# Attention weights turned by 32x32 blocks inside SBUF on SyncE's queue, and queries and keys turned before the values are projected

## The chip, the cores and the metric

One core of one Trainium2 chip runs the whole kernel: TensorE (PE in the profile), VectorE (DVE), ScalarE (ACT), GpSimd (POOL) and SyncE (SP), with 16 DMA engines. SyncE computes nothing here: it issues transfers, in the order in which they stand in its queue, and waits ahead of each for what that transfer needs. GpSimd issues the other transfers in the same manner. The metric is the time of one execution on the device, in microseconds.

## The reference, cut to what matters

One encoder block on 512 tokens (8 rows of 64) of width 1024, all in float32: a half-step SwiGLU feed-forward, a mixer, and a second half-step feed-forward. The mixer projects to seven parts and joins two branches, a gated recurrence and a neighbourhood attention with 16 heads of 64:

```python
xr, gr, q, k, v, ga, gb = jnp.split(h @ w_in[l], splits, axis=-1)
q = _rmsnorm(q.reshape(B_, S, N_HEADS, HEAD_DIM), q_norm[l]) * (HEAD_DIM ** -0.5)
k = _rmsnorm(k.reshape(B_, S, N_HEADS, HEAD_DIM), k_norm[l])
# per row of tokens: an 8 x 32 window of keys for each block of 16 columns, masked to 16
p = jax.nn.softmax(s + bias, axis=-1);  o = p @ v
y = jax.nn.sigmoid(ga) * y_lru + jax.nn.sigmoid(gb) * y_att
x = x + y @ w_out[l]
```

## The kernel before, in words

Every matrix product is made exact enough by splitting both operands into a high and a low part: a block of weights of 512 KB (a chunk) is loaded into `wraw` (three buffers), its high part `wh` is written by ACT or, for every other gate chunk, by DVE (lines 145 and 147), its low part `wl` by DVE (line 148); `wh` and `wl` have four buffers each. A chunk then feeds 24 matmuls of 128x512. So a load can be issued once the chunk three before it has been split, and a chunk can be split once TensorE is done with the chunk four before it. All chunk loads stand on SyncE's queue.

The middle of the kernel goes: projection of xr (8 chunks); then for each half of the heads (hf 0 and 1) a group of 4 chunks for q, 4 for k, 4 for v (24 `wqkv` chunks); then 24 `wg` chunks for the three gates; then 8 `wout` chunks. Each q, k or v group holds all four `acc` banks of PSUM until its results have been copied out: q and k by ACT (line 843), v by DVE (line 856). The next group's matmuls need these banks.

Beside this stream two lanes are woven in, coroutines that advance a few steps after each chunk: the recurrence ("lru") and the attention ("att", the function `heads`). For one half of the heads the attention does the following.

- Norm and turn: the factors `rq` from the sums of squares (lines 894 to 899), then for each of 8 blocks a multiply (904) and a 32x32 block transpose (906) on DVE, and 4 transfers from POOL's queue to DRAM (909): 32 of them in a half.
- `fetch`: reading q and k back in head-major order, as tile `xqk`, on SyncE's queue (917), two transfers for two heads pairs.
- `start(fi)`, for one pair of heads of four: high and low parts of q and k, the last of which is `kl` (939). The scores need it.
- `scores`: 12 matmuls for two of the four column blocks (a unit, n2 = 0 or 1), then on DVE bias and maximum (982), on ACT the exponential (989), on DVE the division (991, 994). In the first half a unit is one step, in the second half both units of a pair go together.
- `ship(fi, n2)`: the weights of a unit have to be transposed for the next matmul. DVE transposes 32x32 blocks into `pt` (1003, 1004; one buffer), one transfer writes `pt` to DRAM as `pd`, and four read it back with blocks exchanged, as `PT` (1006, 1010; three buffers). All five stand on POOL's queue, which waits for the write ahead of the reads.
- `apply(fi)`: 32 matmuls of `PT` with the values (1024), two units after the scores; its result goes to ACT (1034) and, in the gate stage, into y (1103).

The order on every engine is fixed ahead of the run by a list scheduler from the program's order, priorities, and when buffers come free in its own reckoning. On the chip each engine takes its instructions in that order and waits at the first one that is not ready.

Of the kernel before, what the change touches and what calls it, by code (L numbers as in the profile page):

```python
# [9 lines left out]
F32 = mybir.dt.float32  # L10
F32R = mybir.dt.float32r
AF = mybir.ActivationFunctionType
ALU = mybir.AluOpType
# [3 lines left out]
P = 128  # L17
T = 512
# [5 lines left out]
HD = 64  # L24
EPS = 1e-6
ROWS, GW = 8, 64
NCB, QC = 4, 16
# [64 lines left out]
def block_kernel(ctx: ExitStack, tc, a, out):  # L92
    nc = tc.nc
# [3 lines left out]
    big = ctx.enter_context(tc.tile_pool(name="big", bufs=1))  # L97
# [3 lines left out]
    dram = ctx.enter_context(tc.tile_pool(name="dram", bufs=1, space=bass.MemoryType.DRAM))  # L101
# [6 lines left out]
    def nm(s):  # L108
        uid[0] += 1
        return f"{s}_{uid[0]}"  # L110

    NBIG = 43

    def big_t(dt=F32, shape=(P, T), n="b"):
        return big.tile(list(shape), dt, tag="big", bufs=NBIG, name=nm(n))

    def pair_t():
        return big.tile([P, 2, T], F32, tag="pair", bufs=4, name=nm("pair"))
# [132 lines left out]
    def hold(i):  # L251

        after(i, mark["mm"])
        return i
# [12 lines left out]
    def make_forms(xg):  # L267


        half = T // 2  # L270
        F, S = {}, {n: [] for n in FORMS}

        def raw(n, k):
            if k % 2 == 0:
                F[n, k // 2] = big_t(n=n, shape=(P, 2, half))
            x1, x2 = xg[k], xg[k + 4]
            f = F[n, k // 2][:, k % 2]
            if n == "s1":
                sub(f, x2[:, half:], x1[:, half:])
            elif n == "s2":  # L280
                sub(f, F["s1", k // 2][:, k % 2], x1[:, :half], True)
            elif n == "s4":
                sub(f, F["s2", k // 2][:, k % 2], x2[:, :half], True)
            else:
                sub(f, x1[:, :half], x1[:, half:])

        def cut(n):
            H, L = (big_t(F32R, n=n, shape=(P, 2, half)) for _ in range(2))
            mark["cut", n] = split(F[n, len(S[n]) // 2], H, L)
            S[n] += [(H[:, i], L[:, i]) for i in range(2)]  # L290

        return S, raw, cut
# [529 lines left out]
    def tok_group(w, hf):  # L822
        pss = [acc_t() for _ in range(NCB)]
        for kp in range(4):
            H, L = load_w(a["wqkv"][w * 2 + hf, kp], 1024)
            for j in range(NCB):
                tj = slice(j * P, (j + 1) * P)
                for k in range(2):
                    kk = kp * 2 + k
                    s = slice(k * T, (k + 1) * T)  # L830
                    nc.tensor.matmul(pss[j], xh[kk][:, tj], H[:, s], start=kk == 0, stop=False)  # L831
                    nc.tensor.matmul(pss[j], xl[kk][:, tj], H[:, s], start=False, stop=False)  # L832
                    mark["mm"] = nc.tensor.matmul(pss[j], xh[kk][:, tj], L[:, s], start=False, stop=kk == KT - 1)  # L833
            if kp < 3:
                weave(RATE[phase[0]])
        return pss

    def qk_raw(w, hf, st):
        raws = []
        for ps in tok_group(w, hf):  # L840
            t = big_t(n="qk")
            with tc.high_priority():
                copy = nc.scalar.activation(t, ps, AF.Copy)  # L843
            raws.append(t)
        for j, t in enumerate(raws):
            sq = big_t(n="sq")
            after(nc.scalar.activation(sq, t, AF.Square), copy)
            nc.vector.reduce_sum(st[:, w, j, :], sq.rearrange("p (h d) -> p h d", d=HD), axis=AX.X)
        weave(RATE[phase[0]])
        return raws  # L850

    def v_get(hf):
        for j, ps in enumerate(tok_group(2, hf)):
            t = big_t(n="v")
            with tc.high_priority():
                nc.vector.tensor_scalar(t, ps, rcol[:, j : j + 1], None, ALU.mult)
            V[hf, 2 * j] = t

        for j in range(NCB):
            nc.gpsimd.dma_start(vd[hf][:, j * QC : (j + 1) * QC, :], V[hf, 2 * j])  # L860
        for j in range(3):
            t = big_t(n="vs")
            nc.gpsimd.dma_start(t, vd[hf][:, j * QC + 8 : j * QC + 24, :])
            V[hf, 2 * j + 1] = t


        for n, (own, single) in EDGE.items():
            ta, te = big_t(n="va"), big_t(n="ve")
            nc.gpsimd.memset(te, 0.0)
            for h in range(2):  # L870
                for t, half, g in ((ta, 0, own[h][0]), (ta, 1, own[h][1]), (te, h, single)):
                    c = KSTART[n] + g * 8
                    nc.gpsimd.dma_start(
                        t[half * HD : (half + 1) * HD].rearrange("p (f h d) -> p f h d", h=2, d=HD)[:, :, h],
                        vd[hf][:, c : c + 8, :].rearrange("r c (f h d) -> r c f h d", h=2, d=HD)[:, :, :, h])
            V[hf, "own", n], V[hf, "single", n] = ta, te
        weave(RATE[phase[0]])
# [8 lines left out]
            if g == 0:  # L886
                after(ld, mark["xr"])

    def heads(hf, raws, st):

        xs = {}
        qd = [dram.tile([P, NCB, NCB, P], F32, tag="qd", bufs=4, name=nm("qd")) for _ in range(2)]
        rq = tiny.tile([P, 2, NCB, 8], F32, tag="rq", name=nm("rq"))
        for w in range(2):
# [2 lines left out]
                                             ALU.mult, ALU.add))  # L897
        hold(nc.scalar.activation(rq, rq, AF.Sqrt))
        nc.vector.reciprocal(rq, rq)
        yield  # L900
        for w in range(2):
            for j in range(NCB):
                t = raws[w][j].rearrange("p (h d) -> p h d", d=HD)
                hold(nc.vector.tensor_tensor(t, t, rq[:, w, j, :].unsqueeze(2).to_broadcast([P, 8, HD]), ALU.mult))
                t2 = big_t(n="qkt")
                nc.vector.transpose(
                    t2.rearrange("p (c f i) -> p f c i", c=NCB, i=32), raws[w][j].rearrange("p (f c i) -> p f c i", c=NCB, i=32))
                for ab in range(NCB):
                    nc.gpsimd.dma_start(
                        qd[w].rearrange("(c i) j a x -> j a i c x", c=NCB)[j, ab],  # L910
                        t2[ab * 32 : (ab + 1) * 32].rearrange("p (c x) -> p c x", c=NCB))
            yield

        def fetch(g):
            for w in range(2):
                x = big.tile([P, 16, 2, 32], F32, tag="xqk", bufs=2, name=nm("xqk"))
                nc.sync.dma_start(
                    x.rearrange("p x f i -> p x (f i)"), qd[w].rearrange("p j a (g x) -> g p (j a) x", g=2)[g])
                for f in range(2):
                    xs[w, g * 2 + f] = x[:, :, f]  # L920

        yield
        fetch(0)
        yield
        qk, rss, soft, PTs = {}, {}, {}, {}
# [71 lines left out]
        def ship(fi, n2):  # L997

            outer, inner = soft.pop((fi, n2))
            t = big.tile([P, NCB, 7, 32], F32, tag="pt", bufs=1, name=nm("pt"))  # L1000
            sub = lambda b, n: b[:, : n * P].rearrange("p (q c i) -> p q c i", q=n, i=32)
            to = t.rearrange("p c q i -> p q c i")
            nc.vector.transpose(to[:, 4:], sub(outer, 3))
            nc.vector.transpose(to[:, :4], sub(inner, 4))
            d = dram.tile([P, NCB, 7 * 32], F32, tag="pd", bufs=4, name=nm("pd"))
            nc.gpsimd.dma_start(d, t.rearrange("p c q i -> p c (q i)"))
            PT = big.tile([P, NCB, 7, 32], F32, tag="PT", bufs=3, name=nm("PT"))
            for j in range(4):
                q = slice(j * 32, (j + 1) * 32)
                nc.gpsimd.dma_start(PT[:, j].rearrange("p q i -> p (q i)"), d[q].rearrange("i c x -> c i x"))  # L1010
            PTs[fi, n2] = PT.rearrange("p a q i -> p q a i")

        def apply(fi, behind=None):
# [30 lines left out]
        for i in range(len(units) + LC):  # L1044
            behind = None
            if i < len(units):
                fi, n2s = units[i]
                behind = scores(fi, n2s)
            if i >= LC and 1 in units[i - LC][1]:
                apply(units[i - LC][0], behind)  # L1050
            if i < len(units):
                for n2 in n2s:
                    ship(fi, n2)
                if 0 in n2s:
                    if fi < 3:
                        start(fi + 1)
                    if hf * 4 + fi + 1 < KT:
                        bias(hf * 4 + fi + 1)
            yield
            if phase[0] == "g":  # L1060
                yield
                yield
# [4 lines left out]
    for hf in range(2):  # L1067
        st = tiny.tile([P, 2, NCB, 8], F32, tag="st", name=nm("st"))
        raws = [qk_raw(0, hf, st), qk_raw(1, hf, st)]
        v_get(hf)  # L1070
        lanes["att"].append(heads(hf, raws, st))
        phase[0] = "t1" if hf == 0 else "g"


# [144 lines left out]
```

## Time and profile before

| | |
|---|---|
| Three runs | 1209.34, 1210.40, 1210.51 us; median 1210.4 us |
| Profiled execution | 1211.51 us, of which the span is 1209.7 us |
| Busy: PE, PE weight loads, DVE, ACT, POOL | 1112.6, 983.2, 823.9, 582.4, 197.6 us |
| Mean granted clock of TensorE | 0.953 of full |
| Queues | SP's 32.3% of the 16 engines' time, POOL's 23.0% |

Times in the trace are counted from the span's start. Both feed-forward blocks, 0 to about 350 us and from 864 us on, keep TensorE busy nearly without a gap. The mixer lies between them. A busy TensorE can run at half clock, which the column PEclk of the windows shows.

### The profile page before, as it was taken

The numbers are of one execution on the slowest core, as the hardware profiler recorded it, in microseconds if no ns is written. First come the engines' busy times: TensorE is split into PE (matmuls) and PEld (weight loads), VectorE is DVE, ScalarE is ACT, GpSimd is POOL, SyncE is SP. The second block draws the span as 40 slices with busy tenths as digits, with TensorE's granted clock in tenths as the row PEclk, the third lists the DMA queues.
The fourth block names the chain that finished last, engine by engine and source line by source line (L and its number), as shares of the span: only waits on it lengthen the run. The fifth ranks groups of instructions, "written<-read, shape, count | busy, mean of one in ns | idle before, by whom it ended". The sixth has DMA issues, their size and how long they took to land. (4 is left out here: it accounts for less than half of the span.)

```text
span 1209.7 us, 17700 instructions
## 1 busy us (share of the span) xinstructions
PE 1112.6 (92%) x6747; PEld 983.2 (81%) x6747; DVE 823.9 (68%) x1312; ACT 582.4 (48%) x874; POOL 197.6 (16%) x331
## 2 busy tenths in 40 slices
PE   9999999999999999897869962468999999999998
PEld 8899999988887788686658852356999999998887
DVE  7777878866558679966456586424987777775552
ACT  8545454644436697643333224214655454554340
POOL 0000000000003403713532052330100000000000
PEclk9999999999999999899879985588999999999999
DMA  8566666634236947658455365355766666663330
GB/s 269 151 157 158 157 158 157 162 100 132 81 112 161 259 117 228 165 165 233 134 150 167 106 188 136 92 167 147 181 189 161 152 163 153 162 172 108 100 110 35
DMA packets 82149, 184.33 MB, mean 152 GB/s; under 512 B 32656, under 2 KB 36496, under 8 KB 82064
## 3 DMA queue, kind: packets, MB, share of 16 engines
q1 hardware_dynamic: 56256, 122.50, 32.3%
q0 software_dynamic: 25232, 60.44, 23.0%
q8 instruction: 53, 0.87, 0.3%
q10 hardware_dynamic: 576, 0.26, 0.1%
q14 instruction: 32, 0.26, 0.1%
HBM read 154.72 MB, written 19.92 MB: 144 GB/s over the span
## 5 line engine op out<-in xcount | busy, mean ns | idle before, releaser
L145 ACT ACTIVATE wh<-wraw 128x1024 fp32r<-128x1024 f32 (+3 forms) x224 | 220.7, 988 | 344.0 <-issue 98.9
L148 DVE TENSOR_TENSOR wl<-wraw,wh 128x1024 fp32r<-128x1024 f32 (+3 forms) x236 | 267.3, 1137 | 109.5 <-ACT wh L145 108.4
L312 PE MATMUL acc<-s,wh 128*128 128x256 f32 x1280 | 232.2, 283 | 0.0
L312 PEld LDWEIGHTS acc<-s,wh 128*128 128x128 f32 x1280 | 199.7, 192 | 0.0
L312 PE MATMUL acc<-s,wl 128*128 128x256 f32 x640 | 181.1, 283 | 0.0
L312 PEld LDWEIGHTS acc<-s,wl 128*128 128x128 f32 x640 | 122.9, 192 | 0.0
L172 PE MATMUL acc<-xh,wh 128*128 128x512 f32 x272 | 109.6, 403 | 0.0
L174 PE MATMUL acc<-xh,wl 128*128 128x512 f32 x272 | 108.3, 398 | 0.0
L173 PE MATMUL acc<-xl,wh 128*128 128x512 f32 x272 | 108.1, 397 | 0.0
L312 PE MATMUL acc<-xh,wl 128*128 128x256 f32 x320 | 90.6, 283 | 0.0
L312 PE MATMUL acc<-xl,wh 128*128 128x256 f32 x320 | 90.6, 283 | 0.0
L312 PE MATMUL acc<-xh,wh 128*128 128x256 f32 x320 | 90.5, 283 | 0.0
L831 PE MATMUL acc<-wh,xh 128*128 128x512 f32 x192 | 76.5, 399 | 4.9 <-ACT qk L843 4.9
L832 PE MATMUL acc<-wh,xl 128*128 128x512 f32 x192 | 75.7, 394 | 0.0
L833 PE MATMUL acc<-wl,xh 128*128 128x512 f32 x192 | 75.6, 394 | 0.0
L148 DVE TENSOR_TENSOR hl<-h,hh 128x512 fp32r<-128x512 f32 x88 | 57.2, 687 | 21.8 <-PE aux L173 21.5
L172 PE MATMUL aux<-hh,wh 128*128 128x512 f32 (+1 forms) x181 | 69.9, 386 | 0.0
L173 PE MATMUL aux<-hl,wh 128*128 128x512 f32 (+1 forms) x181 | 69.9, 386 | 0.0
L174 PE MATMUL aux<-hh,wl 128*128 128x512 f32 (+1 forms) x181 | 69.9, 386 | 0.0
L173 PE MATMUL acc<-hl,wh 128*128 128x512 f32 (+1 forms) x176 | 67.9, 386 | 0.0
L174 PE MATMUL acc<-hh,wl 128*128 128x512 f32 (+1 forms) x176 | 67.9, 386 | 0.0
L172 PE MATMUL acc<-hh,wh 128*128 128x512 f32 (+1 forms) x176 | 67.9, 386 | 0.0
(222 smaller groups left out, 2374.1 us busy)
## 6 DMA issues: line engine op xcount, KB each, us to landing
wraw<-wqkv SPq DMA_DIRECT2D x24, 512.0 KB, 5.3
wraw<-wg SPq DMA_DIRECT2D x24, 512.0 KB, 3.9
wraw<-w1d SPq DMA_DIRECT2D x22, 512.0 KB, 3.7
wraw<-w2s SPq DMA_DIRECT2D x22, 512.0 KB, 4.2
pair<-w2s SPq DMA_DIRECT2D x22, 512.0 KB, 5.3
wraw<-w2d SPq DMA_DIRECT2D x22, 512.0 KB, 3.6
wraw<-w1s SPq DMA_DIRECT2D x18, 512.0 KB, 4.0
pair<-w1s SPq DMA_DIRECT2D x18, 512.0 KB, 5.5
```

The source lines that it names most:

```text
L145: nc.scalar.activation(H, raw, AF.Copy)
L148: return nc.vector.tensor_tensor(L, raw, H.bitcast(F32), ALU.subtract)
L172: nc.tensor.matmul(ps, wh, xh, start=first, stop=False, skip_group_check=skip)
L173: nc.tensor.matmul(ps, wh, xl, start=False, stop=False, skip_group_check=skip)
L174: mark["mm"] = nc.tensor.matmul(ps, wl, xh, start=False, stop=last, skip_group_check=skip)
L312: mm = nc.tensor.matmul(o, w_[:, c], x_, start=first and m + k == 0 and w_ is H and x_ is xh_, stop=m + k == 4 and w_ is L, skip_group_che ...
L831: nc.tensor.matmul(pss[j], xh[kk][:, tj], H[:, s], start=kk == 0, stop=False)
L832: nc.tensor.matmul(pss[j], xl[kk][:, tj], H[:, s], start=False, stop=False)
L833: mark["mm"] = nc.tensor.matmul(pss[j], xh[kk][:, tj], L[:, s], start=False, stop=kk == KT - 1)
```

## The change: what it does

- `ship` no longer goes through DRAM. The 4x4 grid of 32x32 blocks is exchanged by 16 transfers from SBUF to SBUF, each of 32 partitions by 224 values (28 KB), on SyncE's queue instead of POOL's five. There are 16 units in the kernel, so 256 such transfers take the place of 80. `ship` is given high priority.
- Norm, turn and store of q and k leave the coroutine and stand, as `turn_qk`, ahead of the projection of v; the multiplies lose the tie (`hold`) that kept them behind the newest matmul. `heads` begins with `fetch` and so needs three steps fewer before its first scores.
- New tiles: 43 shared tiles of 2 KB become 38; eight slots of 4 KB ("quad") hold, one after the other in the program, the split forms of the feed-forward, the first half's raw q and k, `xqk`, `pt` and `PT`, which had 2, 1 and 3 buffers of their own.

```diff
-    NBIG = 43
+    NBIG = 38
...
+    def quad_t(shape, dt=F32, n="quad"):
+        return big.tile(list(shape), dt, tag="quad", bufs=8, name=nm(n))
...
         def cut(n):
-            H, L = (big_t(F32R, n=n, shape=(P, 2, half)) for _ in range(2))
+            t = quad_t((P, 2, 2, half), F32R, n)
+            H, L = t[:, 0], t[:, 1]
...
     def qk_raw(w, hf, st):
         raws = []
-        for ps in tok_group(w, hf):
-            t = big_t(n="qk")
+        for j, ps in enumerate(tok_group(w, hf)):
+            if hf == 1:
+                t = big_t(n="qk")
+            else:
+                if j % 2 == 0:
+                    both = quad_t((P, 2, T), n="qk")
+                t = both[:, j % 2]
...
-    def heads(hf, raws, st):
-
-        xs = {}
+    def turn_qk(raws, st):
+
         qd = [dram.tile([P, NCB, NCB, P], F32, tag="qd", bufs=4, name=nm("qd")) for _ in range(2)]
...
         nc.vector.reciprocal(rq, rq)
-        yield
         for w in range(2):
             for j in range(NCB):
                 t = raws[w][j].rearrange("p (h d) -> p h d", d=HD)
-                hold(nc.vector.tensor_tensor(t, t, rq[:, w, j, :].unsqueeze(2).to_broadcast([P, 8, HD]), ALU.mult))
+                nc.vector.tensor_tensor(t, t, rq[:, w, j, :].unsqueeze(2).to_broadcast([P, 8, HD]), ALU.mult)
...
-            yield
+        return qd
+
+    def heads(hf, qd):
+
+        xs = {}
...
-                x = big.tile([P, 16, 2, 32], F32, tag="xqk", bufs=2, name=nm("xqk"))
+                x = quad_t((P, 16, 2, 32), n="xqk")
...
-        yield
         fetch(0)
...
         def ship(fi, n2):
...
-            t = big.tile([P, NCB, 7, 32], F32, tag="pt", bufs=1, name=nm("pt"))
+            t = quad_t((P, NCB, 7, 32), n="pt")
...
-            d = dram.tile([P, NCB, 7 * 32], F32, tag="pd", bufs=4, name=nm("pd"))
-            nc.gpsimd.dma_start(d, t.rearrange("p c q i -> p c (q i)"))
-            PT = big.tile([P, NCB, 7, 32], F32, tag="PT", bufs=3, name=nm("PT"))
-            for j in range(4):
-                q = slice(j * 32, (j + 1) * 32)
-                nc.gpsimd.dma_start(PT[:, j].rearrange("p q i -> p (q i)"), d[q].rearrange("i c x -> c i x"))
+            PT = quad_t((P, NCB, 7, 32), n="PT")
+            for i in range(4):
+                for j in range(4):
+                    nc.sync.dma_start(PT[i * 32 : (i + 1) * 32, j], t[j * 32 : (j + 1) * 32, i])
...
                 for n2 in n2s:
-                    ship(fi, n2)
+                    with tc.high_priority():
+                        ship(fi, n2)
...
         raws = [qk_raw(0, hf, st), qk_raw(1, hf, st)]
+        qd = turn_qk(raws, st)
         v_get(hf)
-        lanes["att"].append(heads(hf, raws, st))
+        lanes["att"].append(heads(hf, qd))
```

The scheduler's order changes with it, at three places above all. Numbers behind names count tiles and differ between the two programs.

DVE, in the first half, up to the copy of the first value tile out of PSUM (line 856 before, 865 now). Before:

```order
L148 TENSOR_TENSOR wl_4940<-wraw_4938,wh_4939 128x1024
L148 TENSOR_TENSOR wl_4977<-wraw_4975,wh_4976 128x1024
L773 SCALAR_TENSOR_TENSOR gate_4277<-gate_4276,gate_4277 128x512
L773 SCALAR_TENSOR_TENSOR gate_4286<-gate_4285,gate_4286 128x512
L773 SCALAR_TENSOR_TENSOR gate_4357<-gate_4356,gate_4357 128x512
L148 TENSOR_TENSOR wl_5025<-wraw_5023,wh_5024 128x1024
L856 TENSOR_SCALAR v_4881<-acc_4700,rcol_3719 128x512
```

Now:

```order
L911 TENSOR_TENSOR qk_4619<-qk_4619,rq_4690 128x512
...
L913 STREAM_TRANSPOSE qkt_4751<-qk_4619 128x4x4x32
...
L151 TENSOR_TENSOR wl_5117<-wraw_5115,wh_5116 128x1024
...
L788 SCALAR_TENSOR_TENSOR th_4456<-gate_4268,gate_4269 128x512
L768 TENSOR_TENSOR gate_4674<-gate_4674,xc_4115 128x512
L790 SCALAR_TENSOR_TENSOR th_4461<-gate_4277,gate_4278 128x512
L768 TENSOR_TENSOR gate_4683<-gate_4683,xc_4115 128x512
L794 TENSOR_TENSOR th_4456<-th_4456,th_4461 128x512
L788 SCALAR_TENSOR_TENSOR th_4504<-gate_4348,gate_4349 128x512
L865 TENSOR_SCALAR v_4938<-acc_4757,rcol_3711 128x512
```

Counted from the split of the third value chunk, that split included, 19 DVE instructions stood ahead of the first value copy before, and 56 stand there now: the 8 multiplies and 8 transposes of `turn_qk`, 8 small ones and a reciprocal for `rq`, one more split, and eleven more of the recurrence.

SP, where the first gate chunks are loaded. Before, the loads stood between reads of q and k:

```order
L163 DMA wraw_5530<-wqkv 128x1024
L163 DMA wraw_5656<-wg 128x1024
L163 DMA wraw_5688<-wg 128x1024
L917 DMA xqk_5271<-qd_5006 128x16x64
L163 DMA wraw_5720<-wg 128x1024
```

Now they stand behind 64 block transfers, those of the first four units, and the last block of the second unit (`PT_5345`) stands at their very end, behind all of the fourth unit's (`PT_5567`):

```order
L1018 DMA PT_5567<-pt_5564 32x224 x12
L1018 DMA PT_5432<-pt_5429 32x224
...
L1018 DMA PT_5567<-pt_5564 32x224
L1018 DMA PT_5345<-pt_5342 32x224
L166 DMA wraw_6015<-wg 128x1024
L166 DMA wraw_6047<-wg 128x1024
L166 DMA wraw_6079<-wg 128x1024
L166 DMA wraw_6184<-wg 128x1024
```

On DVE the splits of these first four gate chunks, with the last transposes of the second half's q and k between them, now stand ahead of the softmax of the fifth unit:

```order
L151 TENSOR_TENSOR wl_6017<-wraw_6015,wh_6016 128x1024
...
L150 CAST wh_6185<-wraw_6184 128x1024
L913 STREAM_TRANSPOSE qkt_5626<-qk_5491 128x4x4x32
L151 TENSOR_TENSOR wl_6186<-wraw_6184,wh_6185 128x1024
L913 STREAM_TRANSPOSE qkt_5633<-qk_5493 128x4x4x32
...
L992 ISA so_5734,nmx_5735<-aux_5718,bm_5457 128x192
```

PE, at the end of the attention. Before, the last `apply` (with `PT_7247` and `PT_7257`) stood among the first matmuls of `wout`, and all of the second half's scores behind 22 of the 24 gate chunks:

```order
L174 MATMUL acc_7391<-yh_6740,wl_7394 128x512
L172 MATMUL acc_7391<-yh_7150,wh_7393 128x512
L1024 MATMUL aux_7361<-PT_7247,va_5578 64x128 x2
L1024 MATMUL aux_7361<-PT_7247,ve_5579 64x128 x2
L1024 MATMUL aux_7361<-PT_7247,vs_5572 64x128 x2
L1024 MATMUL aux_7361<-PT_7247,vs_5574 64x128 x2
L173 MATMUL acc_7391<-yl_7151,wh_7393 128x512
```

Now the second half's scores stand inside gate chunks 11, 13 and 17 and behind chunk 15, and its last `apply` ends behind the first two matmuls of chunk 21 (the rows below, then 22 more matmuls of that chunk and three whole chunks):

```order
L1032 MATMUL aux_7390<-PT_7186,vs_5931 64x128 x2
L1032 MATMUL aux_7390<-PT_7186,vs_5933 64x128 x2
L1032 MATMUL aux_7390<-PT_7186,va_5944 64x128
...
L1032 MATMUL aux_7390<-PT_7186,va_5944 64x128
L1032 MATMUL aux_7390<-PT_7186,ve_5945 64x128 x2
```

The first half's scores move in the same manner: before, the first unit stood behind the second of the four value chunks of the second half, now it stands behind the second half's q group, six chunks earlier, and seven of the eight units stand ahead of the first gate chunk, where three did. Of `apply`, two stand there now and none did.

## The prediction, made before the changed kernel was run

> **What bounds the kernel now.** I read the waits of TensorE first, then its windows stage by stage, then the queues that it waits for. Waits (total us, times, longest):
>
> ```profile
> PE aux L1024 <- DMA PT<-pd: 58.4, 10, 11.6
> PE aux L962 <- DVE kl L939: 27.9, 4, 11.1
> PE acc L831 <- ACT qk L843: 4.9, 1, 4.9
> ```
>
> These 91 us are nearly all that TensorE stands still, and all of it is attention: weights not yet turned, and keys not yet ready for the scores. Windows of the mixer (start:end, length, then busy us of PE, PEld, DVE, ACT, POOL with counts, granted clock, DMA):
>
> ```profile
> 452.00:474.00 22.00, 22.00 (x104) 17.41 (x101) 21.16 (x26) 19.99 (x28) 8.19 (x16) 1.00 0.69 202
> 474.00:501.00 27.00, 24.21 (x107) 19.71 (x105) 26.14 (x43) 18.82 (x25) 13.30 (x20) 1.00 0.70 200
> 501.00:553.00 52.00, 49.89 (x230) 40.36 (x231) 40.18 (x74) 23.93 (x47) 21.65 (x39) 0.93 0.65 168
> 553.00:691.00 138.00, 115.21 (x618) 93.89 (x617) 75.74 (x173) 47.00 (x84) 42.62 (x64) 0.91 0.54 159
> 691.00:720.00 29.00, 22.52 (x100) 18.31 (x98) 27.29 (x41) 9.33 (x12) 17.53 (x32) 0.94 0.65 187
> 720.00:826.00 106.00, 47.63 (x306) 38.81 (x307) 42.96 (x149) 26.86 (x82) 28.31 (x44) 0.64 0.44 122
> ```
>
> Three things are to be seen. From 720 to 826 TensorE works 48 of 106 us, and at a clock of 0.64: there the second half's attention runs alone. From 452 to 501 DVE has no room (47 of 49 us), so anything put ahead in its queue there moves all that follows. In between there are gaps, but milder ones. POOL's queue in the tail shows what one unit costs (start, us, instruction, idle before):
>
> ```profile
> 756.23 0.60 POOL L1006 DMA_DIRECT2D pd<-pt  x1
> 761.67 2.00 POOL L1010 DMA_DIRECT2D PT<-pd  x3 [4.85 <-issue]
> 765.96 0.66 POOL L1010 DMA_DIRECT2D PT<-pd  x1 [2.28 <-issue]
> 766.61 0.60 POOL L1006 DMA_DIRECT2D pd<-pt  x1
> ```
>
> 10.4 us from one write to the next, one unit after the other: eight units make 83 of these 106 us.
>
> **What a unit costs on SyncE's queue.** No row shows this transfer. Its pace is bounded from below by the nearest SyncE rows, back-to-back small loads of 64 KB and loads of 256 KB, and from above by POOL's 32-partition transfers. Then transfers' time from issue to landing (KB each, median us):
>
> ```profile
> 7.62 2.81 SPq L446 DMA_DIRECT2D wraw<-w1gu  x6
> 10.48 0.90 SPq L635 DMA_DIRECT2D pair<-x  x2
> 502.16 15.34 POOL L909 DMA_DIRECT2D qd<-qkt  x28
> out<-o SPq DMA_DIRECT2D x2, 128.0 KB, 1.7
> gate<-pair POOLq DMA_DIRECT2D x64, 128.0 KB, 5.7
> xqk<-qd SPq DMA_DIRECT2D x8, 512.0 KB, 5.9
> wraw<-wg SPq DMA_DIRECT2D x24, 512.0 KB, 3.9
> ```
>
> 2.81/6 = 0.47 and 0.90/2 = 0.45 us each on SP, 0.55 on POOL. I take 0.45, since it is SP that issues, and 2 us to land (SP's small store: 1.7). The other SBUF-to-SBUF transfer, POOL's, takes 5.7; the order lets about eight SP transfers be open at once, so 5.7 to land would mean 5.7/8 = 0.71 each. Range 0.45 to 0.71. At 0.45 a unit takes 16 x 0.45 = 7.2 and 2 to land, 9.2 us: hardly less than 10.4. So the gain can't come from the turn itself; it has to come from the places to which units move, where TensorE has other work. All 256 transfers occupy SP for 115 us, and chunk loads stand behind them.
>
> The Trainium skill, "DMA: Bandwidth & Descriptors", section "Rules for kernel authors", speaks against the change: many small transfers should be joined, since below 64 KB one pays mostly overhead. These are 28 KB. By its fit in "Anatomy of one DMA" (2.0 us and the bytes, for the POOL kind) each would cost 2.0 us to land, and eight open at once 0.25 us each, so that the issue would set the pace; landing in SP's row, 1.7, agrees with it, POOL's 5.7 does not.
>
> **Unit prices for the sum.** Matmuls, scores, an `apply`, and the clock after a gap:
>
> ```profile
> 545.02 0.39 PE L962 MATMUL aux<-kl,qh 64*128 64x256 f32 x2
> 545.95 0.50 PE L831 MATMUL acc<-wh,xh 128*128 128x512 f32 x1
> 552.55 0.49 PE L172 MATMUL acc<-xh,wh 128*128 128x512 f32 x1
> 566.39 0.39 PE L962 MATMUL aux<-kl,qh 64*128 64x256 f32 x2
> 503.11 0.79 PE L831 MATMUL acc<-wh,xh 128*128 128x512 f32 x1 [4.90 <-ACT qk L843]
> 823.41 1.12 PE L1024 MATMUL aux<-PT,vs 128*64 128x128 f32 x8 [4.31 <-DMA PT<-pd]
> 825.31 0.80 PE L174 MATMUL acc<-yh,wl 128*128 128x512 f32 x1
> 828.04 0.63 PE L174 MATMUL acc<-yh,wl 128*128 128x512 f32 x1
> 828.47 0.63 PE L172 MATMUL acc<-yh,wh 128*128 128x512 f32 x1
> 829.51 0.39 PE L172 MATMUL acc<-yh,wh 128*128 128x512 f32 x1
> 829.74 0.40 PE L173 MATMUL acc<-yl,wh 128*128 128x512 f32 x1
> ```
>
> A unit's scores take 0.93 us (545.02 to 545.95). 60 matmuls from 552.55 to 566.39 are 0.23 each, so a chunk is 5.5 us. Half an `apply` takes 1.9 us at half clock, so a whole one 1.9 at full clock. After a gap matmuls come every 0.43 us instead of 0.23 for some 8 of them: a long gap costs 1.6 us more than it lasts.
>
> **The change, place by place,** against the trace of before.
>
> Place one, value copies of the first half. DVE reaches the split of the third value chunk at 456.14 and the first copy at 473.45:
>
> ```profile
> 456.14 1.22 DVE L148 TENSOR_TENSOR wl<-wraw,wh 128x1024 fp32r<-128x1024 f32 x1
> 459.07 0.69 DVE L778 TENSOR_TENSOR gate<-gate,th 128x512 f32<-128x512 f32 x1
> 459.68 0.69 DVE L790 TENSOR_TENSOR th<-th,th 128x512 f32<-128x512 f32 x1
> 461.41 1.20 DVE L786 TENSOR_TENSOR_SCAN th<-gate,gate 128x512 f32<-128x512 f32 x1
> 462.53 1.21 DVE L148 TENSOR_TENSOR wl<-wraw,wh 128x1024 fp32r<-128x1024 f32 x1
> 473.45 1.41 DVE L856 TENSOR_SCALAR v<-acc,rcol 128x512 f32<-128x512 f32 x2
> ```
>
> Start to start, an instruction of 512 elements takes 0.61, a scan 1.12, a split about 1.13. Now 56 instructions stand there: 6 splits 6.8, 7 scans 7.9, 34 of 512 elements 20.7, nine small ones about 1.7 (an estimate from their size): 37.1, so the first copy comes at 493, the banks are free at 494, and the next q group, which began at 474, waits 20 us. Nothing covers it: TensorE has no other bank. Its 4 chunks, the clock's 1.6 and the first scores end at 494 + 22 + 1.6 + 0.9 = 518.5, where TensorE began the k group at 503.1 (the row above, behind the wait for ACT, which falls away). **Lost so far 15 us.**
>
> Place two, up to the first gate matmul, 552.55 before. Now 8 chunks (44), six units (5.6) and two `apply` (3.8) make 53: 572. But `PT_5345`, wanted at about 569, lands with the fourth unit: its scores at 544, some 16 us on a full DVE to 561, 25 transfers of 0.45, landing: 574. Then gate loads: issued at 573, landed at 577 (3.9), split at 579; the fourth chunk's buffer is free only now, so it lands at 583 to 584, is split at 586.5, three transposes to 588.5. Only then comes the softmax of the fifth unit, whose scores were there at 557:
>
> ```profile
> L982 DVE CUSTOM_DVE_ANT_0 so<-aux,bm 128x256 f32<-128x256 f32 x24 | 10.0, 416 | 0.0
> L989 ACT ACTIVATE p<-so,nmx 128x256 f32<-128x256 f32 x32 | 15.9, 496 | 6.9 <-DVE nmx L982 6.8
> ```
>
> Four reductions of 0.4 and four exponentials of 0.5 partly behind them, the divisions and one more transpose, an estimate of 5.5 us. Then `kl` of the fourth pair is ready at 596 and, behind the sixth unit's reductions, the second half's value copies. TensorE waits through it: scores at 596, banks at 599. First gate matmul at **599.5, 47 us behind before.** If DVE or SP were early everywhere this could be 574.
>
> Place three, gates and `wout`, 552.55 to 863.7 before (the chain's first piece of the second feed-forward):
>
> ```profile
> 863.70 5.75 PE acc L312 x48
> ```
>
> 311 us for 768 matmuls (176), 13 units and 8 `apply` (27): 108 us of gaps and slow clock. Now 768 matmuls (176), 9 units (8.4) and 6 `apply` (11.4): 196. Gaps that I find by walking SP and DVE: `xqk` for the last two pairs stands behind 32 transfers (14.4 us) and takes 5.9, so the third pair's scores wait 5; the second and third pair's 64 transfers stand ahead of chunks 19 and 20, so `apply` and chunk 19 wait 11; the last 32 stand ahead of chunk 21, 7; clock after these 3, end of y 2. Sum 196 + 28 = 224, the second feed-forward at 823.5 instead of 863.7. **Gained 40 us in all**: 87 in this place, 47 lost ahead of it.
>
> The feed-forwards I leave at nothing: TensorE never waits there, and five fewer tiles stand against 16 that the split forms no longer take. POOL loses its tail work, which hides nothing now.
>
> Profiled 1211.5 - 40 = 1171.5; the median of the runs lies 1.1 below the profiled execution, so **1170 us**. Its own range: 153 of the 256 transfers stand in these waits (25 in place two, 4 x 32 in place three), so 0.55 a transfer, POOL's pace, would add 15; the two long waits of places one and two could each be off by 8: 1152 to 1196.
>
> **The rivals.**
> - Little is lost in places one and two: DVE's queue has slack that I count as full, or ACT covers it. For it: DVE has slack in 501 to 553 (busy 40 of 52). Against it: 47 of 49 us before. Without the 20 and the 27 us: 1125.
> - SP's pace decides, and it turns out slower than before. At 0.71 us, each of the 153 costs 0.26 more: 40 us, the whole gain, about 1210; at 0.8, about 1224. From 0.72 on it is slower. For it: POOL's 5.7 us for SBUF to SBUF, and loads of 512 KB in the same queue ahead of the small ones. Against it: 0.45 to 0.47 in all SP rows and 1.7 for a small store.
> - The units move but the wait for turned weights stays as long as before in the tail, since 9.2 is hardly less than 10.4: then place three gains only the 28 us of waits for `kl` and what the clock loses, and place two's 47 stay lost: about 1225. Against it: 94 gate matmuls and all of `wout` now stand behind the last `apply`, and gate chunks between the scores.
>
> **How the numbers follow.** The forecast, 1152 to 1196: 0.68. Little lost: 0.14. SP slow: 0.10, of which a fifth lands within 0.2% of before. The old wait stays: 0.08. The range 1132 to 1204 leaves out about a tenth on each side. Faster by over 0.2% (what a measurement of this kernel can tell from no change): 0.68 + 0.14 + a few hundredths of the slow cases near 1200, 0.85; within 0.2%: 0.02; slower: 0.13.
>
> **What would show it.** Right: a wait of some 20 us of the first L831-kind matmul of the second half for the value copy at about 474; one of about 20 us near 577 that names `kl` or the value copies; SP issuing `PT<-pt` 0.45 us apart; no stretch from 720 on with TensorE below half busy; first gate matmul near 600, second feed-forward near 823. Wrong: SP 0.6 us or more apart, or landing over 4 us; gate chunks waiting for `wraw` again and again; no wait at 474; a feed-forward that is longer.

## The result, and the profile after

The changed kernel takes **1197.3 us** (median of 4 runs, 1196.6 to 1201.2) where the kernel before takes 1210.5 beside it (4 runs): the ratio is **0.9898, 95% interval 0.9875 to 0.9921**. It is faster by 13 us, not by the 40 forecast. The profiled execution has a span of 1195.6 us (1209.7 before) and a clock of 0.964 (0.953).

The waits of TensorE after the change (total us, times, longest):

```profile
PE aux L1032 <- DMA PT<-pt: 27.4, 5, 14.0
PE acc L835 <- DVE v L865: 17.1, 1, 17.1
PE aux L972 <- DVE kl L949: 12.5, 2, 10.7
PE aux L1032 <- DVE nmx L992: 9.8, 1, 9.8
PE acc L835 <- ACT qk L852: 4.8, 1, 4.8
PE acc L175 <- ACT hh L148: 2.1, 1, 2.1
```

The waits for turned weights and for keys have fallen from 86 to 40 us, and new ones have come: 17.1 for the value copies, 9.8 for DVE's maxima (`nmx`), and 2.1 in the first feed-forward (`hh`). The same stretches of the mixer as in the prediction (columns as there):

```profile
452.00:474.00 22.00, 22.00 (x107) 17.18 (x106) 22.00 (x36) 20.26 (x30) 4.12 (x8) 1.00 0.52 144
474.00:501.00 27.00, 9.90 (x39) 7.80 (x38) 27.00 (x40) 9.46 (x13) 23.90 (x44) 0.70 0.82 229
501.00:553.00 52.00, 48.10 (x251) 38.70 (x249) 38.35 (x86) 34.96 (x63) 13.18 (x20) 0.99 0.57 148
553.00:691.00 138.00, 115.88 (x608) 93.72 (x609) 84.86 (x201) 47.29 (x99) 36.47 (x61) 0.90 0.54 154
691.00:720.00 29.00, 18.33 (x105) 15.55 (x105) 18.29 (x61) 9.86 (x31) 1.08 (x2) 0.77 0.38 95
720.00:826.00 106.00, 85.43 (x437) 68.95 (x434) 58.04 (x105) 33.80 (x59) 0.89 (x1) 0.89 0.42 131
```

From 720 to 826 TensorE now works 85 of 106 us at a clock of 0.89, where it worked 48 at 0.64. From 474 to 501 it works 9.9 instead of 24.2, while DVE has not a moment free (27.00 of 27.00). From 691 to 720 it works 18 of 29 us. TensorE's timeline shows where it stands still (the longer waits and the first gate matmul, L175 at 604.72); in brackets, the idle time ahead of the instruction and what ended it:

```profile
498.14 0.77 PE L835 MATMUL acc<-wh,xh 128*128 128x512 f32 x1 [17.10 <-DVE v L865]
553.91 0.79 PE L835 MATMUL acc<-wh,xh 128*128 128x512 f32 x1 [4.81 <-ACT qk L852]
...
596.68 0.69 PE L1032 MATMUL aux<-PT,va 128*64 128x128 f32 x4 [9.82 <-DVE nmx L992]
604.72 0.80 PE L175 MATMUL acc<-xh,wh 128*128 128x512 f32 x1 [0.83 <-DVE v L865]
630.13 0.44 PE L1032 MATMUL aux<-PT,va 128*64 128x128 f32 x4 [3.31 <-DMA PT<-pt]
660.39 0.44 PE L1032 MATMUL aux<-PT,va 128*64 128x128 f32 x4 [3.14 <-DMA PT<-pt]
714.55 0.58 PE L972 MATMUL aux<-kl,qh 64*128 64x256 f32 x2 [10.67 <-DVE kl L949]
753.27 0.69 PE L1032 MATMUL aux<-PT,va 128*64 128x128 f32 x4 [14.02 <-DMA PT<-pt]
776.70 0.69 PE L1032 MATMUL aux<-PT,va 128*64 128x128 f32 x4 [4.63 <-DMA PT<-pt]
```

The chain of waits has its first piece of the second feed-forward, at 863.70 before, here:

```profile
849.55 5.75 PE acc L316 x48
```

The second feed-forward begins 14.1 us earlier and takes as long as before to the end (1195.6 - 849.55 = 346.0; 1209.7 - 863.70 = 346.0). The first one does not. The first matmul of the first q group, before and now:

```profile
403.77 0.39 PE L831 MATMUL acc<-wh,xh 128*128 128x512 f32 x1
408.36 0.39 PE L835 MATMUL acc<-wh,xh 128*128 128x512 f32 x1
```

It comes 4.6 us later. At 305 TensorE waits 2.1 us for `hh`, high parts of the feed-forward's hidden values: ScalarE began six of them at 298.67 before, and now begins the first of this stretch at 304.64, behind its steps for the mixer's input (`xh`, `xsq`). Behind the wait some matmuls come 0.43 us apart instead of 0.23. All the runs of the block with the shared tiles show this wait. So the mixer itself gains 18.7 us, of which the first feed-forward takes 4.6 away. SyncE's queue in the mixer (start, us, instruction, count):

```profile
549.36 31.80 SPq L1018 DMA_DIRECT2D PT<-pt  x48
581.20 13.36 SPq L166 DMA_DIRECT2D wraw<-wg  x7
...
685.77 20.43 SPq L1018 DMA_DIRECT2D PT<-pt  x32
706.30 2.14 SPq L928 DMA_DIRECT2D xqk<-qd  x2
708.54 45.10 SPq L1018 DMA_DIRECT2D PT<-pt  x64
```

and this transfer's own durations on it (ns: shortest, median, longest), then its time from issue to landing (us):

```profile
L1018 SPq DMA_DIRECT2D PT<-pt x256: 507/589/3069, 535.2 to 775.4; - x128
...
DMA to landing us min/median/max: 1.7/1.9/9.3
```

20.43/32 = **0.64 us** from one transfer to the next, 45.10/64 = 0.70, where 0.45 was taken. The median duration makes 32 x 0.589 = 18.9 of those 20.43 us: the issuing itself fills the stretch. The loads of the third and fourth pairs' q and k come at 706.30, behind 32 transfers, and TensorE waits 10.7 us for the third pair's keys; 64 transfers fill 708.54 to 753.6, and the `apply` at 753.27 waits 14.0 us.

### The profile page after: what moved, and what is told of

Read it like the earlier page. It is cut to its first block, busy times and chain, and to the rows that moved or that the text cites. A ratio compares the mean times of both kernels' runs of the same rounds, so it can differ in the third digit from the quotient of the medians.

```text
span 1195.6 us, 17835 instructions
## 1 busy us (share of the span) xinstructions
PE 1114.3 (93%) x6747; PEld 982.8 (82%) x6747; DVE 821.7 (69%) x1312; ACT 581.4 (49%) x872; POOL 144.4 (12%) x251
## 4 chain that ended last, share of the span: by engine, by line
PE 77%; SPq 10%; DVE 6%; DMA 3%; issue 2%; ACT 2%; DVEq 0%; ACTq 0%
PE acc L316 29%; SPq L1018 10%; PE acc L176 7%; PE acc L177 7%; PE acc L175 7%; PE aux L316 5%; PE aux L176 3%; PE aux L177 3%; PE aux L175 3%; PE acc L835 2%; PE acc L836 2%; PE acc L837 2%; DVE wl L151 1%; DMA xqk<-qd 1%; DMA wraw<-wg 1%
## 5 line engine op out<-in xcount | busy, mean ns | idle before, releaser
L175 PE MATMUL acc<-xh,wh 128*128 128x512 f32 x272 | 108.8, 400 | 2.7 <-ACT wh L148 1.9
L835 PE MATMUL acc<-wh,xh 128*128 128x512 f32 x192 | 78.3, 408 | 21.9 <-DVE v L865 17.1
L175 PE MATMUL aux<-hh,wh 128*128 128x512 f32 (+1 forms) x181 | 70.0, 387 | 0.0
L175 PE MATMUL acc<-hh,wh 128*128 128x512 f32 (+1 forms) x176 | 67.9, 388 | 2.1 <-ACT hh L148 2.1
```

The costliest lines, as they stand in the source:

```text
L175: nc.tensor.matmul(ps, wh, xh, start=first, stop=False, skip_group_check=skip)
```

## The experiments

The theory: the term that failed is SyncE's pace, and the units' new places bring what was forecast. The rivals: landing or the chain through DVE sets the end, not the issue; the gain comes from the turn inside SBUF, not from the move; the losses of places one and two are larger than their price.

**The pace by itself.** The kernel leaves out the block and issues only families of small transfers. The first three families, on three queues, overlap in time; from 25.93 us on all the rows below have SyncE's queue alone.

> This kernel leaves out the whole block: it only issues families of 16 small transfers on an idle core, so that only its trace is read. In the trace of the changed kernel a transfer of 32 partitions x 896 bytes from SBUF to SBUF takes 0.589 us on SyncE's queue (median of 256) and lands after 1.9 us, while a load of 512 KB takes 0.328 us. Theory (the pace of the queue's own issue decides, whatever else runs): on the idle core each of the 16 takes 0.59 us again, 0.60 to 0.70 from one to the next, and lands in 1.5 to 2 us. Rival (what else is in flight slows them, landings hold them back): on the idle core they take 0.33 and stand 0.35 to 0.45 apart, as predicted. Open, and to be read: whether the same transfer on ScalarE's and GpSimd's queues, between the same partitions, with 128 partitions of 224 bytes, to and from DRAM, or with four times the bytes takes as long.

SyncE's queue in the trace (digits at the end of names are cut off): L112 is the changed kernel's own transfer, first as it is, then between the same partitions; L133 the same bytes as 128 partitions by 224 bytes; the next two go to DRAM and from DRAM; L147 has four times the bytes, and L159 448 KB in 128 partitions. The last row is ScalarE's queue.

```profile
2.23 10.25 SPq L112 DMA_DIRECT2D sp_ss<-src  x16
15.87 7.47 SPq L112 DMA_DIRECT2D sp_ss32same<-pool_ss  x12
25.93 8.83 SPq L133 DMA_DIRECT2D sp_ss<-sp_ss32same  x14
37.30 5.85 SPq L112 DMA_DIRECT2D sp_sd<-sp_ss  x12
43.20 7.52 SPq L112 DMA_DIRECT2D sp_ds<-sp_sd  x16
52.63 8.77 SPq L147 DMA_DIRECT2D sp_ss32big<-sp_ds  x14
74.64 2.99 SPq L159 DMA_DIRECT2D sp_ss128big<-sp_t  x4
4.54 10.20 ACTq L112 DMA_DIRECT2D act_ss<-sp_ss  x16
```

Without the kernel around it the pace is again 10.25/16 = 0.64, and landing takes 1.9. Between the same partitions it is 0.62; with 128 partitions and with 112 KB, where no other queue works, it is 0.63: the rival, that traffic slows the transfers, falls. On ScalarE's queue it is 0.64, while SyncE's works too. Between 28 and 112 KB neither size nor shape matters; four transfers of 448 KB (L159) took 0.75 each. With DRAM on one side the transfer of 28 KB takes 0.49 and 0.47. That is the prediction's 0.45 to 0.47, whose rows were all loads from DRAM.

**Half of the transfers on ScalarE's queue.**

```diff
-                    nc.sync.dma_start(PT[i * 32 : (i + 1) * 32, j], t[j * 32 : (j + 1) * 32, i])
+                    eng = nc.scalar if j % 2 else nc.sync
+                    eng.dma_start(PT[i * 32 : (i + 1) * 32, j], t[j * 32 : (j + 1) * 32, i])
```

> Of each unit's 16 transfers 8 go to ScalarE's queue; everything else is as in the changed kernel, and the order on TensorE nearly so. Theory (the pace of SyncE's queue is the term that was mis-sized): a unit takes SyncE 8 x 0.63 = 5 us instead of 10; the waits for PT in the second half (3.3 + 3.1 + 14.0 + 4.6 us) fall to about 10, the wait of 10.7 us for the fourth pair's keys, whose load stands behind 32 transfers, by about 10, and the gate loads are issued 8 us earlier: 1170 to 1180 us. Rival (not SyncE's pace but the chain softmax, transposes, landing, or ScalarE, which now issues for 128 x 0.6 = 77 us): no change within 5 us, or slower, 1195 to 1215.

Measured 1171.4 us, ratio 0.967 (0.964 to 0.970), 26 us below the changed kernel: the theory's range. The wait for the third pair's keys is 5.6 instead of 10.7, the longest for `PT` 6.7 instead of 14.0. It has a price: ScalarE's own work now stands behind the transfers in its queue (its waits in this kernel):

```profile
ACT p L999 <- DMA PT<-pt: 24.5, 3, 12.1
ACT pair L1096 <- DMA PT<-pt: 23.9, 3, 10.1
```

**All of them on GpSimd's queue** (`nc.sync` becomes `nc.gpsimd` in the line above).

> All 16 transfers of a unit go to GpSimd's queue, which is empty in the second half; the order on TensorE stays nearly the same. Theory (SyncE's queue is held for 10 us per unit, and loads of keys and of gate chunks stand behind): these loads are early again, the wait of 10.7 us for keys goes and the gate loads come at about 573 instead of 581; a unit itself takes 16 x 0.55 and 3 to 6 us to land, 12 to 15 us, so that the waits for PT stay or grow by 2 to 3 us each: 1180 to 1198 us. Rival (landing decides: 5.7 us for GpSimd's other SBUF-to-SBUF transfer, eight open at once): 17 us for a unit, 1210 or more.

Measured 1172.7 us, ratio 0.9677 (0.9646 to 0.9708): more gain than the theory allowed, against the rival. The transfers' durations and landing here:

```profile
L1018 POOL DMA_DIRECT2D PT<-pt x256: 496/496/966, 535.2 to 760.3; - x128
...
DMA to landing us min/median/max: 1.6/2.5/6.3
```

and one unit on that queue's timeline:

```profile
568.55 8.42 POOL L1018 DMA_DIRECT2D PT<-pt  x16 [1.41 <-DMA PT<-pt]
```

GpSimd is quicker at issuing them (8.42/16 = 0.53 us) and they land in 2.5 us, not 5.7. The wait for keys of 10.7 becomes 2.8 at most. What is left is one wait of 12.3 us at 671, for a unit whose transfers on GpSimd's queue stood behind the value loads that it issues from 618 to 650.

**Place one: the value copies on ScalarE.**

```diff
-                nc.vector.tensor_scalar(t, ps, rcol[:, j : j + 1], None, ALU.mult)
+                nc.scalar.activation(t, ps, AF.Copy, scale=rcol[:, j : j + 1])
```

> The value copies (L865) go from DVE to ScalarE; nothing else changes. Theory (place one as predicted: the value copy stands behind 56 instructions on DVE, TensorE waits 17.1 us for it, and ScalarE has room, 9.5 busy of 27 us there): the wait at 498 goes, TensorE begins the next group at 481 to 484, and some of it is lost again where the units come due no earlier, in place two: 1183 to 1192 us. Rival (DVE has the same work to do and everything behind it waits for DVE and SyncE anyway): the gain of place one is taken back in place two, 1194 to 1200.

Measured 1187.6 us, ratio 0.9798 (0.9765 to 0.9831), as the theory has it. TensorE's order in the trace is the same, but for a few missing records, and it begins the group at 483.68 instead of 498.14:

```profile
483.68 0.80 PE L835 MATMUL acc<-wh,xh 128*128 128x512 f32 x1 [3.08 <-ACT v L865]
593.53 0.79 PE L175 MATMUL acc<-xh,wh 128*128 128x512 f32 x1 [0.78 <-ACT v L865]
```

Of the 14.5 us gained there 11.2 are left at the first gate matmul (604.72 before this edit).

**The change in two halves.** First the move alone: `turn_qk` stays ahead of the values, and the weights go through DRAM on GpSimd's queue, with the lines of the kernel before.

> The move of turn_qk stays, the weights are turned as before: one store to DRAM and four loads on GpSimd's queue, 10.4 us from one unit to the next in the trace of before. Theory (the gain comes from where the units stand, the turn on SyncE's queue costs more than the old one): SyncE is free for the loads of keys and gate chunks as when GpSimd issues all 16 (1172.7 us), and a unit is some 2 us longer than the 8 to 9 us that those 16 took from issue to issue: 1165 to 1190 us, at any rate below the changed kernel's 1197. Rival (the gain comes from the turn SBUF to SBUF): the move alone leaves the old waits for turned weights, 1200 to 1225.

Then the turn alone: `heads` takes back the norm, the turn and the store, with its `hold` and its yields; the 16 transfers and the shared tiles stay.

> The weights are turned SBUF to SBUF on SyncE's queue with the shared tiles, but normalising, turning and storing of q and k goes back into the attention's steps, where it was before. Theory (16 x 0.63 and 2 to land, 12.2 us, is longer than the 10.4 of before, and the units start as late as before): place one has no wait of 17 us, but the second half's units stand one behind the other in the tail with each nearly 2 us longer and the chunk loads of the gates and of wout stand behind them: 1212 to 1235 us, slower than before. Rival (it is the turn that gains): at or below 1197.

The move alone: 1192.0 us, ratio **0.9816** (0.9794 to 0.9838). The turn alone: 1222.7, ratio **1.0082** (1.0066 to 1.0098). 0.9816 x 1.0082 = 0.9897, and both together measured 0.9898. As run, the move is worth 22 us and the turn takes 10 back. That the product agrees so closely is in part chance: both halves keep the shared tiles and the raised priority, and in both the first q group begins some 4 us late (407.45 and 407.86), a loss that the product counts twice. Without it the move would be worth some 26 us and the turn would cost some 6 (estimates: 22 + 4 and 10 - 4). The signs stay. The move alone came out 2 us above the theory's range; one wait is enough to account for that, on TensorE's timeline:

```profile
659.77 0.69 PE L1034 MATMUL aux<-PT,va 128*64 128x128 f32 x4 [26.85 <-DMA PT<-pd]
```

and on GpSimd's:

```profile
642.19 0.77 POOL L882 DMA_DIRECT2D ve<-vd  x1
...
644.62 0.56 POOL L1017 DMA_DIRECT2D pd<-pt  x1
```

The unit's weights were in `pt` by 625, but its store stands on GpSimd's queue behind the value loads (L882), as with all 16 transfers on that queue, and leaves at 644.62. With the turn alone the wait is for keys, which TensorE's timeline shows first, and SyncE's queue behind it: 32 transfers stand ahead of the keys' loads.

```profile
768.15 0.58 PE L971 MATMUL aux<-kl,qh 64*128 64x256 f32 x2 [25.34 <-DVE kl L948]
```

```profile
739.25 20.47 SPq L1017 DMA_DIRECT2D PT<-pt  x32
759.82 2.06 SPq L926 DMA_DIRECT2D xqk<-qd  x2
```

**Five transfers instead of 16 on SyncE's queue, through DRAM** (one store, four loads, as before, but `nc.sync`; the move stays).

> The move stays; a unit's weights go through DRAM on SyncE's queue with one store and four loads. On the idle core the store took SyncE 0.80 us and landed after 3.0, the four loads took 2.38: some 3.2 us of the queue's time per unit instead of 10. Theory (the queue's time per transfer decides): the waits that it makes for keys and chunks shrink, a unit takes 3.2 and two landings of 2.5 to 3, some 8.5 us instead of 12.2, but the loads wait in the queue for the store and hold what is behind: 1160 to 1180 us. Rival (the landing decides, not the issue): two landings instead of one cost what the issue saves, 1190 to 1205.

Measured 1186.6 us, ratio 0.978 (0.9765 to 0.9794): between the two, so neither is the whole. The queue issues less, but it stands at the loads (L1020) until the store has landed, 77.3 us in all, and what is behind stands with it. From the waits of SyncE's queue, and of TensorE:

```profile
SPq L1020 <- DMA pd<-pt: 77.3, 16, 9.4
```

```profile
PE aux L1034 <- DMA PT<-pd: 27.1, 7, 9.4
```

The Trainium skill, "DMA: Bandwidth & Descriptors", section "Rules for kernel authors", which the prediction set against the change, advises joining small transfers. This run does that and gains 11 us on the changed kernel, so the measurement agrees with it in sign; but the weights also go through DRAM again, which the run does not separate, and the next two runs, with transfers of 28 KB, gain more.

**Half on GpSimd's queue**, alone, and together with the value copies on ScalarE:

```diff
-                    nc.sync.dma_start(
+                    (nc.gpsimd if j % 2 else nc.sync).dma_start(
```

> Half of each unit's 16 transfers on GpSimd's queue, the value copies on DVE as in the changed kernel: the part of the best version that was not yet run alone. With both together the time was 1140.9 us, 57 below the changed kernel, while half on ScalarE's queue (26) and the value copies on ScalarE (10) make 36. Theory (ScalarE's own issuing, 0.64 us each with waits for free tiles in front of its evictions, ate part of the gain there, GpSimd has nothing to lose): 1150 to 1160 us, so that the two parts add up again. Rival (the parts only gain so much together, since what place one gains is lost again while SyncE is late): 1168 to 1175, as with ScalarE or with all on GpSimd.

> Two changes that gained are put together: the value copies on ScalarE (10 us alone) and half of each unit's 16 transfers on a second queue, here GpSimd's, which has no other work in the second half (half on ScalarE's alone gained 26 us). Theory (they act in different places, 474 to 501 and from 540 on, and add up): 1197 - 26 - 10 = 1161, range 1154 to 1168 us. Rival (both gains are one and the same slack on SyncE and DVE): no better than one of them, 1170 to 1187.

Alone it measures 1150.0 us, ratio **0.9488** (0.9468 to 0.9507); with the value copies 1140.9, ratio 0.9397 (0.9372 to 0.9422), better than the 1154 to 1168 expected. From 0.9898 to 0.9488 is 0.041 of 1211, 50 us (47 between the medians): the two remedies do add up (50 and about 11). That ScalarE's own work ate half the gain in its run fits the waits shown there, but GpSimd also issues faster, and no run separates the two. With half on GpSimd, TensorE has no gap from 720 to 826 (the second feed-forward begins at 802):

```profile
720.00:826.00 106.00, 106.00 (x608) 91.36 (x608) 78.19 (x112) 55.50 (x76) 9.97 (x16) 1.00 0.63 176
```

By the prediction's own rule, 153 transfers on the path, halving 0.64 is worth 153 x 0.32 = 49. The agreement proves little, since the same rule gives as much for half on ScalarE's queue, which gained 26. One thing goes along and was not separated: with fewer transfers on the queue the scheduler also puts gate loads between the first four units, four of them here and five with half on ScalarE's, so they are issued from 543 on instead of from 581. GpSimd's queue has its price too, once more for a unit behind the value loads (TensorE, half on GpSimd's queue alone):

```profile
642.98 0.70 PE L1032 MATMUL aux<-PT,va 128*64 128x128 f32 x4 [7.69 <-DMA PT<-pt]
```

**The raised priority of `ship`**, taken away from the changed kernel and from the best one.

```diff
-                    with tc.high_priority():
-                        ship(fi, n2)
+                    ship(fi, n2)
```

> The changed kernel without the raised priority of a unit's transposes and transfers. In the changed kernel SyncE's queue mixes the transfers of two or three units, so that the first one's weights land with the last one's: 64 transfers stand ahead of the apply that waits 14.0 us, 45 ahead of the one that waits in the first half. Without the priority each unit's 16 stand together. Theory (each transfer ahead of the one that is wanted costs 0.63): the waits for PT (27.4 us in all) fall by 5 to 12 us, those for keys, whose load stays behind 32 transfers, don't: 1185 to 1193 us. Rival (the priority brings the units forward, without it their transposes stand behind the chunks' splits on DVE): 1200 to 1212.

> The best version so far (value copies on ScalarE, half of the transfers on GpSimd's queue, 1140.9 us) without the raised priority. With 8 transfers of a unit on SyncE the queue's order differs from it in few rows. Theory: within 8 us of it, 1133 to 1149, lower if the order of the transfers still made the wait of 11.8 us for PT at 632. Rival: the priority matters more where the queue is no longer the limit, 1150 to 1165.

The first measures 1198.7 us, ratio 0.9883 (0.9858 to 0.9907): no difference, outside of both expectations. Its first gate matmul comes at 594.18, 10 us earlier than with the priority, but the third pair's scores begin at 714.60, where they began at 714.55: the 10 us have gone by then, above all in two waits of TensorE. SyncE's queue reaches the loads for these keys at 706.26, as with the priority (706.30); why it comes no earlier the runs do not show.

```profile
630.39 1.12 PE L1032 MATMUL aux<-PT,vs 128*64 128x128 f32 x8 [8.18 <-DMA wraw<-wg]
714.60 0.58 PE L972 MATMUL aux<-kl,qh 64*128 64x256 f32 x2 [14.26 <-DVE kl L949]
```

```profile
706.26 2.06 SPq L928 DMA_DIRECT2D xqk<-qd  x2
```

The second measures **1133.7 us**, ratio **0.9355** (0.9319 to 0.9390), the fastest of all; its interval overlaps with that of the version with the priority.

## Why the prediction was right or wrong, point by point

- **What bounds the kernel, and where the gain comes from: right.** Not the turn but the places of the units: the move alone gains 22 us, the turn alone loses 10. The tail is filled (48 to 85 of 106 us).
- **Place one: right.** The value copy was put at 493 and the next group at 494 after a wait of 20; measured 497.3 and 498.1 after 17.1. The group before it ends at 476 in the trace of before, not at 474, and everything is late by the first feed-forward's 4.6. The k group begins 19.6 us behind before (522.75 and 503.11); without the 4.6 that is 15.0, and 15 was forecast. Moving the copies to another engine removes the wait, which shows its cause.
- **Place two: right to 1 us, with some luck.** First gate matmul at 599.5 forecast, 604.7 measured; 47 us behind forecast, 52 measured, of which 4.6 are the first feed-forward's. The gate loads are issued at 581 instead of 573, 4 us of it because of the transfers ahead, and the chain behind them is 3 us shorter than forecast. It ends with DVE's reductions and `kl`, as forecast, in a wait of 9.8 us and two short ones instead of one of about 20. The 4.8 us for ScalarE's copies, which was to fall away, stands ahead of the v group now, at 553.91.
- **The step that failed: "Range 0.45 to 0.71. At 0.45 a unit takes 16 x 0.45 = 7.2 and 2 to land, 9.2 us".** The landing is right (1.9). The pace is 0.64: 10.2 and 2, 12.2 us, longer than the old 10.4. The text chose the low end "since it is SP that issues", but its rows were loads from DRAM, and the probe shows that a transfer with SBUF on both sides takes this queue 0.16 us longer. No row of before showed that.
- **Place three: its mechanism right, its size wrong.** Forecast 224 us from the first gate matmul to the second feed-forward, measured 849.6 - 604.7 = 245. The waits that were named are there: 5 for the keys behind 32 transfers became 10.7; 11 behind 64 became 14.8; 7 for the last 32 became 5.8 (the last two with the short wait for a split right behind them). Two of 3 us had not been seen, and slow clock with the rest took 11 instead of 5. So 15 of the 21 us are waits for what comes through SyncE's queue, and 6 are clock and rest.
- **A second step that failed: "The feed-forwards I leave at nothing: TensorE never waits there".** For the second one that is right, to 0.1 us. The first one lost 4.6 us, with a wait of 2.1. The prediction looked at the tiles and not at ScalarE's order; which of the new tiles moved that order the runs do not separate.
- **The sum.** The second feed-forward begins 26 us later than forecast: 4.6 of it come from the first feed-forward, under 1 from places one and two, 21 from place three. The prediction's own price for the pace gives 128 x (0.64 - 0.45) = 24 us for place three, about what was lost there, so the pace is the larger part of what is missing. With the 25 transfers of place two it gives 29 and 1170 + 29 = 1199 us, measured 1197.3; that this comes so near is in part luck, since it leaves out the 4.6 and place two lost almost nothing. No run had a pace of 0.45, so this share is worked out. What the runs show is that taking half or all of the transfers off SyncE's queue gains 25 to 50 us.
- **The rivals.** "SP's pace decides" was the nearest, in between: by its price 11 of the 40 us are left at 0.64, and 13 were measured. "Little is lost" was wrong by nearly the full 47 us; "the old wait stays" by the filled tail. The estimate that the prediction worked out from the Trainium skill, "DMA: Bandwidth & Descriptors", section "Anatomy of one DMA", was that issue sets the pace and landing takes 2.0 us. The trace agrees: 0.589 of 0.64 us are the issuing, and landing takes 1.9 on SyncE's queue.

## What to carry to other kernels

A queue's time per transfer is a price of its own, like an engine's time per instruction: multiply it by the number of transfers on the path, and take it from a row with the same ends (SBUF or DRAM) on the same queue, or measure it alone first. If no such row exists and the forecast stands or falls with it, put the middle of the bounds into the sum and not the end that suits the mechanism. When a queue has become the bound, look at what stands behind the new transfers (here keys and weight chunks) and split them over a queue that has little else to issue. And read the wait of every engine in the stages that the change is said not to touch: new tiles can change an engine's order there.

## What the runs showed of the hardware

- On SyncE's and ScalarE's queues a transfer from SBUF to SBUF is issued every 0.62 to 0.64 us in the probe, whether of 28 or of 112 KB, of 32 or of 128 partitions, with or without a change of partition; with DRAM on one side a transfer of 28 KB every 0.47 to 0.49.
- GpSimd's queue issues the same transfers every 0.53 us in the kernel, so it is not the slower of the two here, and they land in 2.5 us there. The 5.7 of its 128 KB SBUF-to-SBUF transfers, from which the prediction took its upper bound, does not hold for them.
- A queue that stands at a transfer holds back what is behind it: with half of the transfers on ScalarE's queue its exponentials waited up to 12.1 us; on SyncE's queue the loads behind a store waited 77.3 us in all; on GpSimd's a unit behind the value loads cost TensorE 7.7 us.
